# One 512-column matmul over the high and low half of the activations, and token sections of 256 and 264

## The chip, the cores and the metric

The kernel runs on one core of a Trainium2 chip. Its time is the device time of one execution in microseconds (us). The core has a matmul engine (PE, whose weight loads are shown apart as PEld), a vector engine (DVE), a scalar engine (ACT), a GpSimd engine (POOL) and a queue engine (SP) that starts the DMA transfers. All of them follow their own instruction lists and wait for each other by semaphores.

## The reference, cut to what matters

One layer of a hybrid decoder is run for a prompt of 512 tokens and for 8 sample tokens that share its weights. Everything is float32.

```
h = RMSNorm(x);  z = h @ w_in           # 2048 -> 7168 columns, split among branches
pool branch:   windowed means of u, a 128x128 map per group, gated by silu
dil branch:    3 groups x 4 heads of dilated window attention, QK-norm, merged by denominators
mem branch:    4-head cross-attention into 256 memory tokens (mem @ w_mem_kv, QK-norm)
x = x + concat(branches) @ w_out        # 1536 -> 2048 columns
```

The caches of the sample tokens are copied to the outputs, shifted by one position (most of the DMA traffic).

## The kernel before

The tokens lie along the free axis: 512 prompt and 8 sample tokens are NT = 520 columns, and 128 channels fill the partitions. A *job* computes 128 output channels for all 520 tokens: 56 jobs for w_in (16 blocks of 128 input channels each, "k-steps"), 8 jobs for the memory's keys and values (16 k-steps, 256 columns), and 16 jobs for w_out (12 k-steps).

Float32 precision comes from a split. A weight block `w` and an activation block `x` are each written as a high part, rounded to the matmul engine's reduced float32 (`F32R`), and a low part, the rest. A k-step adds up three products: high weight by high activation, high weight by low activation, low weight by high activation. The tokens are cut into two sections of HT = 260 columns (`SEC`), each with its own PSUM bank, so a k-step has six matmuls of 260 columns, each with its own weight load. The reduced-float32 matmuls have the tile names `whi` and `wlo` in their rows; the attention's own matmuls are in full float32 and run as two passes each.

The weights come as raw tiles (`wraw`) by DMA. `emit_split` cuts them a quarter of a job at a time (4 k-steps): ACT writes `whi`, DVE writes `wlo` from the raw tile and `whi`, both 128x512. Four such pairs are kept, so a quarter is split about three quarters of a job before PE needs it. The activation halves are the tiles `xh0..15` and `xl0..15`; the output projection writes its split activations into the same tiles (`split_y`). The memory's split activations use tiles that are free at that time (`y0..y11`, `S`, `kp`).

When a job's sums are done they are read out of PSUM one k-step into the next job (`flush_pend`, `evac`): per section one DVE instruction, sum times `rs_x` (the RMS factor) for w_in, or sum plus the residual for w_out (`o_evac`, `run_last`), times `rs_m` for the memory. Two PSUM tiles of two banks each (`psum_m`) take turns, so a readout has a whole job of time. The tile framework makes waits by whole tiles: in `run_last`, whose two sections run one after the other in one PSUM tile, the second section's first matmul waits for the readout of the first.

The order of everything is written by the kernel's own planner when it is built. A model of the engines' clocks (`Clock`) is advanced by every instruction; after each k-step `tick` gives the attention, normalization and sample tasks their next pieces as long as the modelled DVE and ACT backlog is under 2.5 us. So the DVE list mixes the weight splits, the readouts and the attention's arithmetic, in one fixed order, and an instruction that waits holds up all that stand behind it. POOL does the sums over partitions (`partition_all_reduce`).

The whole program: load and scale x while jobs 0 and 1 run; four jobs of memory queries and two more; the memory stage (8 jobs, some 45 to 55 us, up to about 155 us); 50 more w_in jobs with the attention of the four heads beside them; 16 output jobs.

Of the kernel before, what the change touches and what calls it, by code (L numbers as in the profile page):

```python
# [10 lines left out]
F32 = mybir.dt.float32  # L11
# [7 lines left out]
P = 128  # L19
# [4 lines left out]
NT = SEQ + NS  # L24
HT = NT // 2
ML = 256
# [88 lines left out]
def trunk(ctx, tc, nc, I, O):  # L115
# [88 lines left out]
    def mm(out, lhsT, rhs, start, stop):  # L204
        nc.tensor.matmul(out, lhsT=lhsT, rhs=rhs, start=start, stop=stop)  # L205
        n = nfree(rhs)
        d = 2 * max(0.107, n / 1200.0) if lhsT.dtype == F32 else max(0.107, (n + 6) / 2400.0)
        ck.use("pe", d, [lhsT, rhs], [out])

    def tr(out, in_):  # L210
# [97 lines left out]
    ysm = st([P, NH, NS], "ysm")  # L308
    xh = [st([P, NT], f"xh{k}", dt=F32R) for k in range(KB)]
    xl = [st([P, NT], f"xl{k}", dt=F32R) for k in range(KB)]  # L310
    Y = {}
# [95 lines left out]
    def run_jobs(group, each=None, before=None):  # L407
        accs = {}
        for j in group:
            _, _, _, sections, _, wide = jobs[j]  # L410
            if wide:
                t = psum_m()
                accs[j] = [t[:, s, 0:c1 - c0] for s, (c0, c1) in enumerate(sections)]
            else:
                need("psb", len(sections))
                accs[j] = [psum_b()[:, 0:c1 - c0] for c0, c1 in sections]
                if len(sections) == 2:
                    accs[j].append(None)
        nkb = jobs[group[0]][1]
        cur = {}  # L420
        for k in range(nkb):
            if before:
                before(k)
            for j in group:
                _, _, lhs, sections, _, _ = jobs[j]
                if k % 4 == 0:
                    cur[j] = split_t.pop((j, k))
                whi, wlo = cur[j]
                mh, ml = lhs(k)
                for a, b, w, m in ((0, 0, whi, mh), (0, 1, whi, ml), (1, 0, wlo, mh)):  # L430
                    for s, (c0, c1) in enumerate(sections):
                        mm(accs[j][s], w[:, k % 4, :], m[:, c0:c1],
                           start=(k == 0 and a == 0 and b == 0), stop=(k == nkb - 1 and a == 1))
            if each:
# [8 lines left out]
        for j in group:  # L443
            pend.append((len(jobs[j][3]) == 2, lambda j=j: jobs[j][4](accs[j])))

    def run_last(j):

# [3 lines left out]
        for s, (c0, c1) in enumerate(SEC):  # L451
            acc = t[:, s, 0:c1 - c0]
            for k in range(KO):
                whi, wlo = split_t[j, k - k % 4]
                mh, ml = xs(k)
                for n, (w, m) in enumerate(((whi, mh), (whi, ml), (wlo, mh))):
                    mm(acc, w[:, k % 4, :], m[:, c0:c1], k == 0 and n == 0, k == KO - 1 and n == 2)
                if k == 0:
                    flush_pend()
            d_tt(o[:, c0:c1], acc, xr[:, c0:c1], ALU.add)  # L460
            store(O["o_y"][j - first_o][:, c0:c1], o[:, c0:c1])
# [33 lines left out]
    def mem_evac(i):  # L495
        h = i % NH

        def key(acc):
            z = kmem[h]
            d_tt(z, acc[0], rs_m, ALU.mult)  # L500
            give("psb")
# [6 lines left out]
        def value(acc):  # L508
            need("vt")
            z = row("vt", 2)[:, 0:ML]  # L510
            d_tt(z, acc[0], rs_m, ALU.mult)
            give("psb")
# [17 lines left out]

    SEC = ((0, HT), (HT, NT))

    def evac(z, acc):
        for s, (c0, c1) in enumerate(SEC):
            d_tt(z[:, c0:c1], acc[s], rs_x[:, c0:c1], ALU.mult)
        if len(acc) > 2:
# [334 lines left out]
    def pool_task(c, u):  # L871
# [25 lines left out]
        for s, (c0, c1) in enumerate(SEC):  # L897
            mm(a[s][:, 0:HT], poolw[c], nt_[:, c0:c1], True, True)
        give("vt", 2)
# [4 lines left out]
        for s, (c0, c1) in enumerate(SEC):  # L904
            yv = Y[c][:, c0:c1]
            d_stt(yv, a[s][:, 0:HT], gains[:, GC_PS + c:GC_PS + c + 1], yv, ALU.mult, ALU.mult)
        give("psb", 2)
# [26 lines left out]
    def o_evac(m):  # L934
        def f(acc):
            xr = xres.pop(m)
            o = row("tmp", 3)
            for s, (c0, c1) in enumerate(SEC):
                d_tt(o[:, c0:c1], acc[s], xr[:, c0:c1], ALU.add)
            store(O["o_y"][m], o)  # L940
# [5 lines left out]

    xs = lambda k: (xh[k], xl[k])

# [13 lines left out]
    for i in range(NM):  # L962
        job(I["w_mem"][i], KB, lambda k: (memt[k // 2][0][:, k % 2, :], memt[k // 2][1][:, k % 2, :]),
            ((0, ML),), mem_evac(i), False)
# [32 lines left out]
    with tc.manual_schedule():  # L997
# [62 lines left out]
        def mem_prep():  # L1060
# [10 lines left out]
            for i in range(8):  # L1071
                r = raw.pop(i)
                mh = st([P, 2, ML], f"y{i}", 1, F32R)
                if i < 4:
                    ml = st([P, 2, ML], f"y{8 + i}", 1, F32R)
                elif i < 7:
                    if i == 4:
                        mls = st([P, 3, 2, ML], "S", 1, F32R)
                    ml = mls[:, i - 4]
                else:  # L1080
                    ml = st([P, 2, ML], "kp", 1, F32R)
                for s in range(2):
                    k = 2 * i + s
                    g = gains[:, GC_M + k:GC_M + k + 1]
                    act(mh[:, s, :], r[:, s, :], AF.Copy, scale=g)
                    d_stt(ml[:, s, :], r[:, s, :], g, mh[:, s, :].bitcast(F32), ALU.mult, ALU.subtract)
                if i == 0:
                    act(acc_m, r, AF.Square)
                else:
# [4 lines left out]
                    give("tmp")  # L1094
                memt[i] = (mh, ml)
                fetch(i + 4)
# [167 lines left out]
```

## Time and profile before

| what | value |
|---|---|
| median of 3 runs | 928.36 us (927.41 to 928.66) |
| the profiled execution's own time | 927.97 us |
| its span, first to last instruction | 925.7 us |
| PE busy / DVE busy / ACT busy / POOL busy | 893.5 / 666.8 / 393.2 / 311.3 us |
| matmuls recorded | 7208 |
| mean granted TensorE clock | 0.992 of full speed |

"Busy" counts the time in which an engine has at least one instruction in work. Matmuls overlap one another, so a busy PE says only that it has work; how fast it goes is read from how far apart the matmuls start. The columns of the stretch table are the busy times of the engines in one stretch, each with its count of instructions, then the granted clock (1.00 is 2.4 GHz, 0.50 is 1.2 GHz), the busy share of the DMA engines and GB/s.

### The profile page before, as it was taken

To read this page: it belongs to the slowest core of one execution; us is meant where nothing else is said; L and a number is where in the kernel's file an instruction comes from. 1 tells how busy PE (TensorE), PEld (TensorE's weight loads), DVE (VectorE), ACT (ScalarE), POOL (GpSimd) and SP (SyncE) were. 2 spreads that over 40 slices of the span, in tenths; PEclk is the share of its full clock that TensorE was granted. 3 is DMA by queue.
4 is the path that set the end of the run, shared out by engine and by line. 5 is a ranking of instruction groups with operands and counts; after the bars stand their busy time and mean duration, and the time that the engine had idled before them with its cause. 6 is when DMAs were issued, how large, how long until landed. Compare 5 with 4: busy or idle time off the path is not lost.

```text
span 925.7 us, 18086 instructions
## 1 busy us (share of the span) xinstructions
PE 893.5 (97%) x7208; PEld 878.0 (95%) x7208; DVE 666.8 (72%) x1218; ACT 393.2 (42%) x785; POOL 311.3 (34%) x109
## 2 busy tenths in 40 slices
PE   5789998999999999999999999999999999999998
PEld 5689888999999999999999999999999999999998
DVE  7947898846776886798857996798766999533331
ACT  6336565443453453443434454245542535222220
POOL 4612525515333742372422743355323520000000
PEclk9889999999999999999999999999999999999999
DMA  7553356897777686659987689676986757699631
GB/s 241 172 180 130 114 190 193 269 355 236 239 243 249 215 283 198 219 185 309 334 263 257 225 289 337 220 252 214 337 301 210 268 169 252 227 391 320 234 117 47
DMA packets 64643, 219.52 MB, mean 237 GB/s; under 512 B 8488, under 2 KB 22696, under 8 KB 62376
## 3 DMA queue, kind: packets, MB, share of 16 engines
q1 hardware_dynamic: 64560, 218.39, 70.0%
q8 instruction: 56, 0.92, 0.4%
q14 instruction: 27, 0.22, 0.1%
HBM read 200.32 MB, written 106.25 MB: 331 GB/s over the span
## 4 chain that ended last, share of the span: by engine, by line
PE 75%; DVE 6%; ACT 1%; issue 1%; ACTq 0%
PE psm L205 70%; PE psb L205 4%; DVE wlo L164 2%; DVE sv L187 1%; DVE mx L164 1%; PE psb L211 1%; ACT sk L154 0%; DVE sz L164 0%; ACT whi L154 0%; DVE sy L164 0%; DVE qk L164 0%; DVE smx L183 0%; DVE vt L164 0%; DVE smx L168 0%; ACT ss L154 0%
## 5 line engine op out<-in xcount | busy, mean ns | idle before, releaser
L205 PE MATMUL psm<-xh,whi 128*128 128x260 f32 x2120 | 439.6, 288 | 10.2 <-ACT whi L154 7.1
L205 PE MATMUL psm<-xl,whi 128*128 128x260 f32 x2120 | 431.7, 284 | 9.2 <-DVE xl L168 8.7
L205 PE MATMUL psm<-xh,wlo 128*128 128x260 f32 x2120 | 431.6, 284 | 2.3 <-DVE wlo L164 2.3
L164 DVE TENSOR_TENSOR wlo<-wraw,whi 128x512 fp32r<-128x512 f32 x304 | 257.5, 857 | 219.6 <-ACT whi L154 212.8
L154 ACT ACTIVATE whi<-wraw 128x512 fp32r<-128x512 f32 x304 | 188.8, 628 | 403.6 <-PE psm L205 347.7
L205 PEld LDWEIGHTS psm<-xh,whi 128*128 128x128 f32 x2120 | 330.9, 190 | 16.7 <-ACT whi L154 7.1
L205 PEld LDWEIGHTS psm<-xl,whi 128*128 128x128 f32 x2120 | 329.3, 190 | 10.7 <-DVE xl L168 9.8
L205 PEld LDWEIGHTS psm<-xh,wlo 128*128 128x128 f32 x2120 | 330.2, 190 | 2.8 <-DVE wlo L164 2.7
L197 POOL PARTITION_ALL_REDUCE sk<-sk x32 | 132.6, 4145 | 145.0 <-DVE sk L164 105.6
L197 POOL PARTITION_ALL_REDUCE sq<-sq x32 | 104.6, 3276 | 137.8 <-ACT sq L154 137.8
L197 POOL PARTITION_ALL_REDUCE mx<-mx x17 | 44.3, 2605 | 84.8 <-DVE mx L164 82.8
L154 ACT ACTIVATE tmp<-tmp 128x520 f32<-128x520 f32 (+2 forms) x76 | 46.4, 610 | 16.6 <-DVE sq L168 14.4
L154 ACT ACTIVATE sk<-sk,smx 128x256 f32<-128x256 f32 (+1 forms) x64 | 35.2, 550 | 16.5 <-DVE smx L168 14.8
L205 PE MATMUL psb<-y,wlo 128*128 128x256 f32 x128 | 37.0, 289 | 5.2 <-DVE wlo L164 5.0
L205 PE MATMUL psb<-y,whi 128*128 128x256 f32 x192 | 41.1, 282 | 0.9 <-ACT whi L154 0.9
L168 DVE SCALAR_TENSOR_TENSOR qk<-qk,gains_r,sq 128x520 f32<-128x520 f32 x28 | 38.4, 1370 | 1.0
L205 PEld LDWEIGHTS psb<-y,whi 128*128 128x128 f32 x192 | 31.6, 188 | 1.1 <-ACT whi L154 1.1
L154 ACT ACTIVATE sq<-qk 128x520 f32<-128x520 f32 x28 | 17.5, 633 | 34.6 <-DVE qk L164 34.6
L205 PEld LDWEIGHTS psb<-y,wlo 128*128 128x128 f32 x128 | 24.0, 188 | 7.3 <-DVE wlo L164 7.3
L201 POOL TENSOR_TENSOR rsx<-rsx,y 128x520 f32<-128x520 f32 x15 | 24.5, 1633 | 12.4 <-DVE y L164 11.2
L187 DVE CUSTOM_DVE_ANT_1 sv<-sv,sk,sy 128x384 f32<-128x384 f32 x32 | 27.3, 892 | 0.6
L183 DVE TENSOR_REDUCE smx<-sk 128x2 f32<-128x512 f32 (+1 forms) x32 | 25.9, 810 | 0.0
(126 smaller groups left out, 701.5 us busy)
## 6 DMA issues: line engine op xcount, KB each, us to landing
o_cache<-cache SPq DMA_DIRECT2D x88, 712.0 KB, 7.3
wraw<-w_in SPq DMA_DIRECT2D x108, 512.0 KB, 5.3
o_cache<-cache SPq DMA_DIRECT2D x24, 584.0 KB, 6.5
vn<-xT SPq DMA_DIRECT2D x32, 260.0 KB, 4.6
wraw<-w_mem SPq DMA_DIRECT2D x16, 512.0 KB, 3.7
wraw<-w_out SPq DMA_DIRECT2D x14, 512.0 KB, 4.2
o_zero<-zero SPq DMA_DIRECT2D x6, 1024.0 KB, 7.4
sk<-dks SPq DMA_DIRECT2D x16, 384.0 KB, 4.9
```

Source lines behind the costliest of these rows:

```text
L154: nc.scalar.activation(out=out, in_=in_, func=func, scale=scale, bias=bias, **kw)
L164: nc.vector.tensor_tensor(out=out, in0=in0, in1=in1, op=op)
L168: nc.vector.scalar_tensor_tensor(out=out, in0=in0, scalar=scalar, in1=in1, op0=op0, op1=op1)
L183: nc.vector.tensor_reduce(out=out, in_=in_, op=op, axis=axis)
L187: nc.vector.tensor_tensor_reduce(out=out, in0=in0, in1=in1, scale=1.0, scalar=init, op0=op0, op1=op1, accum_out=accum)
L197: nc.gpsimd.partition_all_reduce(t, t, P, op)
L201: nc.gpsimd.tensor_tensor(out=out, in0=in0, in1=in1, op=op)
L205: nc.tensor.matmul(out, lhsT=lhsT, rhs=rhs, start=start, stop=stop)
L211: nc.tensor.transpose(out, in_, ident)
```

## The change

The two halves of an activation block lie in one tile, `xs2[k]` of shape [128, 2, 520], and the memory's in one tile per k-step, `memt[k]`. The sections are 256 and 264 columns. For a section of 256 columns a new helper `mm3` issues one matmul of the high weight over both halves at once: 2 x 256 moving columns, written to 512 columns of one PSUM bank. The low weight's product of 256 columns is added to the first 256 of them. The section of 264 has the three matmuls of before. A k-step has five matmuls (512, 256, 264, 264, 264) and the same 1560 columns. The memory's k-step has two (512 and 256) in place of three.

The two halves of such a sum are added when they are read (`read_acc`): with a residual by two DVE instructions; with a factor by an ACT copy of the second half out of PSUM, a DVE addition of the first half, and a DVE multiplication. The planner's price of a reduced-float32 matmul changes from max(0.107, (n+6)/2400) to (n+28)/2400 us.

```diff
-HT = NT // 2
+LO = 256
...
-        d = 2 * max(0.107, n / 1200.0) if lhsT.dtype == F32 else max(0.107, (n + 6) / 2400.0)
+        d = 2 * max(0.107, n / 1200.0) if lhsT.dtype == F32 else (n + 28) / 2400.0
         ck.use("pe", d, [lhsT, rhs], [out])
+
+    def mm3(accs, whi, wlo, m2, sections, first, last):
+
+
+        for acc, (c0, c1) in zip(accs, sections):
+            n = c1 - c0
+            if n == LO:
+                mm(acc, whi, m2[:, :, c0:c1], first, False)
+                mm(acc[:, 0:n], wlo, m2[:, 0, c0:c1], False, last)
+            else:
+                mm(acc[:, 0:n], whi, m2[:, 0, c0:c1], first, False)
+                mm(acc[:, 0:n], whi, m2[:, 1, c0:c1], False, False)
+                mm(acc[:, 0:n], wlo, m2[:, 0, c0:c1], False, last)
 
     def tr(out, in_):
         nc.tensor.transpose(out, in_, ident)
...
     ysm = st([P, NH, NS], "ysm")
-    xh = [st([P, NT], f"xh{k}", dt=F32R) for k in range(KB)]
-    xl = [st([P, NT], f"xl{k}", dt=F32R) for k in range(KB)]
+    xs2 = [st([P, 2, NT], f"x{k}", dt=F32R) for k in range(KB)]
+    xh = [t[:, 0, :] for t in xs2]
+    xl = [t[:, 1, :] for t in xs2]
     Y = {}
     QKB = 8
     VNB = 6
...
                 t = psum_m()
-                accs[j] = [t[:, s, 0:c1 - c0] for s, (c0, c1) in enumerate(sections)]
+                accs[j] = [t[:, s, :] for s in range(len(sections))]
             else:
                 need("psb", len(sections))
-                accs[j] = [psum_b()[:, 0:c1 - c0] for c0, c1 in sections]
+                accs[j] = [psum_b() for _ in sections]
                 if len(sections) == 2:
                     accs[j].append(None)
         nkb = jobs[group[0]][1]
...
-                mh, ml = lhs(k)
-                for a, b, w, m in ((0, 0, whi, mh), (0, 1, whi, ml), (1, 0, wlo, mh)):
-                    for s, (c0, c1) in enumerate(sections):
-                        mm(accs[j][s], w[:, k % 4, :], m[:, c0:c1],
-                           start=(k == 0 and a == 0 and b == 0), stop=(k == nkb - 1 and a == 1))
+                mm3(accs[j], whi[:, k % 4, :], wlo[:, k % 4, :], lhs(k), sections, k == 0, k == nkb - 1)
             if each:
                 each(k)
             if k % 4 == 3:
...
 
+    def read_acc(out, acc, other, op):
+
+        n = out.shape[-1]
+        if n != LO:
+            d_tt(out, acc[:, 0:n], other, op)
+        elif op == ALU.add:
+            d_tt(out, acc[:, 0:n], other, op)
+            d_tt(out, out, acc[:, n:2 * n], op)
+        else:
+            act(out, acc[:, n:2 * n], AF.Copy)
+            d_tt(out, out, acc[:, 0:n], ALU.add)
+            d_tt(out, out, other, op)
+
...
     def run_last(j):
 
         t = psum_m()
         xr = xres.pop(j - first_o)
         o = row("tmp", 3)
         for s, (c0, c1) in enumerate(SEC):
-            acc = t[:, s, 0:c1 - c0]
+            acc = t[:, s, :]
             for k in range(KO):
                 whi, wlo = split_t[j, k - k % 4]
-                mh, ml = xs(k)
-                for n, (w, m) in enumerate(((whi, mh), (whi, ml), (wlo, mh))):
-                    mm(acc, w[:, k % 4, :], m[:, c0:c1], k == 0 and n == 0, k == KO - 1 and n == 2)
+                mm3([acc], whi[:, k % 4, :], wlo[:, k % 4, :], xs(k), ((c0, c1),), k == 0, k == KO - 1)
                 if k == 0:
                     flush_pend()
-            d_tt(o[:, c0:c1], acc, xr[:, c0:c1], ALU.add)
+            read_acc(o[:, c0:c1], acc, xr[:, c0:c1], ALU.add)
             store(O["o_y"][j - first_o][:, c0:c1], o[:, c0:c1])
 
 
...
             z = kmem[h]
-            d_tt(z, acc[0], rs_m, ALU.mult)
+            read_acc(z, acc[0], rs_m, ALU.mult)
             give("psb")
 
             def after():
...
 
 
-    SEC = ((0, HT), (HT, NT))
+    SEC = ((0, LO), (LO, NT))
 
     def evac(z, acc):
         for s, (c0, c1) in enumerate(SEC):
-            d_tt(z[:, c0:c1], acc[s], rs_x[:, c0:c1], ALU.mult)
+            read_acc(z[:, c0:c1], acc[s], rs_x[:, c0:c1], ALU.mult)
         if len(acc) > 2:
             give("psb", 2)
 
...
             for s, (c0, c1) in enumerate(SEC):
-                d_tt(o[:, c0:c1], acc[s], xr[:, c0:c1], ALU.add)
+                read_acc(o[:, c0:c1], acc[s], xr[:, c0:c1], ALU.add)
             store(O["o_y"][m], o)
             if len(acc) > 2:
                 give("psb", 2)
...
 
-    xs = lambda k: (xh[k], xl[k])
+    xs = lambda k: xs2[k]
 
     def zjob(cb, done, wide=True):
         job(I["w_in"][cb], KB, xs, SEC, done, wide)
...
-        job(I["w_mem"][i], KB, lambda k: (memt[k // 2][0][:, k % 2, :], memt[k // 2][1][:, k % 2, :]),
+        job(I["w_mem"][i], KB, lambda k: memt[k],
             ((0, ML),), mem_evac(i), False)
     first_q = len(jobs)
     for h in range(NH):
...
                 r = raw.pop(i)
-                mh = st([P, 2, ML], f"y{i}", 1, F32R)
-                if i < 4:
-                    ml = st([P, 2, ML], f"y{8 + i}", 1, F32R)
-                elif i < 7:
-                    if i == 4:
-                        mls = st([P, 3, 2, ML], "S", 1, F32R)
-                    ml = mls[:, i - 4]
-                else:
-                    ml = st([P, 2, ML], "kp", 1, F32R)
                 for s in range(2):
                     k = 2 * i + s
+                    if k < 12:
+                        m2 = st([P, 2, ML], f"y{k}", 1, F32R)
+                    elif k < 15:
+                        if k == 12:
+                            mls = st([P, 3, 2, ML], "S", 1, F32R)
+                        m2 = mls[:, k - 12]
+                    else:
+                        m2 = st([P, 2, ML], "kp", 1, F32R)
                     g = gains[:, GC_M + k:GC_M + k + 1]
-                    act(mh[:, s, :], r[:, s, :], AF.Copy, scale=g)
-                    d_stt(ml[:, s, :], r[:, s, :], g, mh[:, s, :].bitcast(F32), ALU.mult, ALU.subtract)
+                    act(m2[:, 0, :], r[:, s, :], AF.Copy, scale=g)
+                    d_stt(m2[:, 1, :], r[:, s, :], g, m2[:, 0, :].bitcast(F32), ALU.mult, ALU.subtract)
+                    memt[k] = m2
                 if i == 0:
                     act(acc_m, r, AF.Square)
                 else:
...
                     give("tmp")
-                memt[i] = (mh, ml)
                 fetch(i + 4)
                 ck.last = max(ck.pe, ck.written[raw[i + 1].tensor.name]) if i < 7 else ck.last
                 yield
```

In `run_last` each section's loop now calls `mm3` with that one section.

The matmul engine's list, in an ordinary w_in job; the rows of one k-step and the start of the next, before and after (`x2` joins equal rows; psm is the PSUM tile, xh, xl and x the activations):

```order
L205 MATMUL psm_7694<-xh_23_86,whi_7576 128x260 x2
L205 MATMUL psm_7694<-xl_39_102,whi_7576 128x260 x2
L205 MATMUL psm_7694<-xh_23_86,wlo_7577 128x260 x2
L205 MATMUL psm_7694<-xh_24_87,whi_7576 128x260 x2
L205 MATMUL psm_7694<-xl_40_103,whi_7576 128x260 x2
```

```order
L205 MATMUL psm_6792<-x_32_95,whi_6728 128x512
L205 MATMUL psm_6792<-x_32_95,wlo_6729 128x256
L205 MATMUL psm_6792<-x_32_95,whi_6728 128x264 x2
L205 MATMUL psm_6792<-x_32_95,wlo_6729 128x264
L205 MATMUL psm_6792<-x_33_96,whi_6728 128x512
```

Six matmuls have become five, and the low weight is wanted after one matmul instead of four.

DVE's list around the readout of the same w_in job (a q or k of the second head's attention), before and after (qk is the readout's target, psm the sums, rsx the RMS factor; mx, S, sk, smx belong to the attention and the sample tokens):

```order
L164 TENSOR_TENSOR wlo_4695<-wraw_4322,whi_4694 128x512
L164 TENSOR_TENSOR wlo_4724<-wraw_4322,whi_4723 128x512
L164 TENSOR_TENSOR qk_4747<-psm_4579,rsx_71 128x260 x2
L164 TENSOR_TENSOR sk_4597<-sk_4597,qs_81 128x768
L164 TENSOR_TENSOR mx_4751<-S_4348 128x512
```

```order
L164 TENSOR_TENSOR mx_4221<-S_3891 128x512
L164 TENSOR_TENSOR mx_4221<-mx_4221,S_3891 128x4x64 x3
L164 TENSOR_TENSOR mx_4221<-mx_4221,S_3891 128x4x32
L183 TENSOR_REDUCE smx_4241<-sk_3413 128x2
L168 SCALAR_TENSOR_TENSOR smx_4241<-smx_4241,nself_3884 128x2
L164 TENSOR_TENSOR wlo_4265<-wraw_3872,whi_4264 128x512
L164 TENSOR_TENSOR qk_4282<-qk_4282,psm_4120 128x256
L164 TENSOR_TENSOR qk_4282<-qk_4282,rsx_71 128x256
L164 TENSOR_TENSOR qk_4282<-psm_4120,rsx_71 128x264
L164 TENSOR_TENSOR sk_4163<-sk_4163,qs_81 128x768
```

The readout has three DVE rows instead of two (its ACT copy stands in ACT's list), and the attention's `mx` rows have moved ahead of it. DVE has 80 instructions more in all (56 + 8 + 16), ACT 64 more (56 + 8).

The end of DVE's list, the readouts of the last two jobs, before and after (tmp is the result tile, vn the residual):

```order
L164 TENSOR_TENSOR tmp_10902<-psm_10804,vn_10722 128x260 x2
L164 TENSOR_TENSOR wlo_10927<-wraw_10681,whi_10926 128x512
L164 TENSOR_TENSOR wlo_10955<-wraw_10746,whi_10954 128x512
L164 TENSOR_TENSOR tmp_10987<-psm_10895,vn_10815 128x260 x2
L164 TENSOR_TENSOR tmp_10983<-psm_10982,vn_10906 128x260 x2
```

```order
L164 TENSOR_TENSOR tmp_9908<-psm_9828,vn_9759 128x256
L164 TENSOR_TENSOR tmp_9908<-tmp_9908,psm_9828 128x256
L164 TENSOR_TENSOR tmp_9908<-psm_9828,vn_9759 128x264
L164 TENSOR_TENSOR tmp_9905<-psm_9904,vn_9839 128x256
L164 TENSOR_TENSOR tmp_9905<-tmp_9905,psm_9904 128x256
L164 TENSOR_TENSOR tmp_9905<-psm_9904,vn_9839 128x264
```

The first section of the last job is read by two instructions, and the second section's matmuls stand behind both.

## Rows read from the trace of the kernel before

**Rows 1.** The page, part 1: busy time of each engine, share, instructions.

```profile
PE 893.5 (97%) x7208; PEld 878.0 (95%) x7208; DVE 666.8 (72%) x1218; ACT 393.2 (42%) x785; POOL 311.3 (34%) x109
```

**Rows 2.** Chain that ended last: start us, length us, engine, tile, instructions.

```profile
156.06 48.29 PE psm L205 x402
...
805.99 111.35 PE psm L205 x929
...
917.36 0.44 DVE tmp L164
...
917.84 4.58 PE psm L205 x36
...
922.45 0.43 DVE tmp L164
```

**Rows 3.** Timeline of PE, memory stage: start us, us, instruction, count.

```profile
121.47 0.28 PE L205 MATMUL psb<-y,wlo 128*128 128x256 f32 x1
...
122.89 0.28 PE L205 MATMUL psb<-y,wlo 128*128 128x256 f32 x1
```

**Rows 4.** Timeline of PE, at half clock.

```profile
34.67 0.64 PE L205 MATMUL psm<-xh,wlo 128*128 128x260 f32 x2
...
37.27 0.42 PE L205 MATMUL psm<-xh,wlo 128*128 128x260 f32 x1
```

**Rows 5.** Stretches: us, PE, PEld, DVE, ACT, POOL busy (count), clock, DMA, GB/s.

```profile
34.30:37.40 3.10, 3.10 (x15) 3.10 (x16) 3.10 (x4) 2.95 (x5) 2.52 (x2) 0.50 0.76 272
...
100.00:160.00 60.00, 52.77 (x420) 50.10 (x420) 55.28 (x91) 34.31 (x68) 29.46 (x9) 1.00 0.54 176
394.00:450.00 56.00, 55.22 (x456) 54.86 (x455) 49.63 (x85) 26.39 (x58) 27.32 (x8) 1.00 0.77 261
520.00:560.00 40.00, 40.00 (x335) 40.00 (x334) 38.36 (x67) 21.49 (x46) 17.51 (x6) 1.00 0.87 296
604.00:660.00 56.00, 54.53 (x451) 54.17 (x450) 49.12 (x95) 26.92 (x60) 26.99 (x7) 1.00 0.72 252
740.00:790.00 50.00, 50.00 (x412) 49.76 (x411) 45.96 (x114) 21.44 (x45) 4.75 (x1) 1.00 0.64 214
800.00:900.00 100.00, 100.00 (x838) 100.00 (x836) 33.53 (x62) 22.73 (x36) 0.00 (x0) 1.00 0.75 265
```

**Rows 6.** Chain, 203 to 208 us: a full-float32 matmul of 512 columns.

```profile
204.35 0.86 PE psb L205 x2
```

**Rows 7.** Waits of PE: who for whom, us in total, times, longest.

```profile
PE psm L205 <- DVE xl L168: 8.7, 5, 2.4
...
PE psb L205 <- DVE wlo L164: 5.0, 8, 1.4
PE psm L205 <- DVE wlo L164: 2.3, 2, 1.5
...
PE psm L205 <- DVE tmp L164: 0.5, 1, 0.5
```

**Rows 8.** Groups by form: shapes, count, busy us, mean ns, idle before.

```profile
L164 DVE TENSOR_TENSOR wlo<-wraw,whi 128x512 fp32r<-128x512 f32 x304 | 257.5, 857 | 219.6 <-ACT whi L154 212.8 <-PE psb L205 2.8 <-DMA wraw<-w_out 2.2
...
L164 DVE TENSOR_TENSOR qk<-psm,rsx 128x260 f32<-128x260 f32 x62 | 23.3, 419 | 0.0
...
L154 ACT ACTIVATE y<-vn,gains 128x256 fp32r<-128x256 f32 x16 | 7.2, 494 | 0.0
...
L164 DVE TENSOR_TENSOR S<-S,mx 128x256 f32<-128x256 f32 x12 | 4.3, 415 | 0.0
```

**Rows 9.** Tile wlo on DVE: ns min/median/max.

```profile
L164 DVE TENSOR_TENSOR wlo<-wraw,whi x304: 674/691/3732, 7.0 to 910.6; 128x512 fp32r<-128x512 f32 x152
```

**Rows 10.** Chain, 630 to 660 us.

```profile
637.01 2.80 DVE wlo L164
...
644.44 0.69 DVE wlo L164
...
645.18 14.92 PE psm L205 x122
```

**Rows 11.** Groups by form, DVE, 800 to 926 us.

```profile
L164 DVE TENSOR_TENSOR wlo<-wraw,whi 128x512 fp32r<-128x512 f32 x40 | 27.5, 692 | 67.3 <-ACT whi L154 63.8 <-DMA wraw<-w_out 2.2 <-PE psb L205 1.3
```

More of the change, by code (lines that the diff above doesn't have):

```diff
@@ L510, in value @@
             z = row("vt", 2)[:, 0:ML]
-            d_tt(z, acc[0], rs_m, ALU.mult)
+            read_acc(z, acc[0], rs_m, ALU.mult)
             give("psb")
@@ L897, in pool_task @@
         for s, (c0, c1) in enumerate(SEC):
-            mm(a[s][:, 0:HT], poolw[c], nt_[:, c0:c1], True, True)
+            mm(a[s][:, 0:c1 - c0], poolw[c], nt_[:, c0:c1], True, True)
         give("vt", 2)
@@ L905, in pool_task @@
             yv = Y[c][:, c0:c1]
-            d_stt(yv, a[s][:, 0:HT], gains[:, GC_PS + c:GC_PS + c + 1], yv, ALU.mult, ALU.mult)
+            d_stt(yv, a[s][:, 0:c1 - c0], gains[:, GC_PS + c:GC_PS + c + 1], yv, ALU.mult, ALU.mult)
         give("psb", 2)
```

## The prediction

> **What bounds the kernel now.** I read the page's busy times first, then the chain of waits, then the stretches, then who waits for whom. PE is busy 893.5 of 925.7 us, the next engine, DVE, 666.8 [rows 1]. The chain shows why that is no idle figure: from 156 us on it is matmuls end to end, 402 in 48.29 us, and near the end 929 in 111.35 us [rows 2]. That is 120.1 and 119.9 ns from one 260-column matmul to the next. At the full clock of 2.4 GHz the 260 columns alone are 108.3 ns, so each matmul has 11.5 ns on top. A step of six takes 6 x 119.9 = 719 ns.
>
> Three places are not paced by PE. At the start it waits for x (8.7 us in five waits for `xl`) [rows 7]. In the memory stage DVE is busy 55.28 of 60 us and PE waits eight times, 5.0 us, for `wlo` [rows 5, 7]. And in four stretches of the attention (394 to 450, 520 to 560, 604 to 660, 740 to 790 us) DVE is busy 88 to 96% of the time [rows 5]: there a weight split comes late, as at 644.44, right after which PE goes on at 645.18 [rows 10]. Over 800 to 900 us DVE has only 33.53 us of work [rows 5].
>
> **The change, part by part.** I start from the profiled execution, 927.97 us; the median is 0.4 above it.
>
> *PE after the memory stage.* Columns per k-step stay at 6 x 260 = 512 + 256 + 3 x 264 = 1560. Matmuls go from six to five. What this saves depends on what the 11.5 ns belong to, and no row before shows a 512-column matmul of this kind.
> - If they belong to the matmul, whatever its length, a step saves 11.5 ns. The 256-column matmuls speak for it: 12 of them in 122.89 - 121.47 = 1.42 us, 118.3 ns each, or 106.7 + 11.6 [rows 3].
> - If they belong to the column, PE streams 260/119.9 = 2.17 columns per ns, and the step saves nothing. 256/118.3 = 2.16 fits this as well; four columns are too few to tell the two apart.
> - If a longer stream hides them, 512 columns cost little over 213.3 ns. The nearest row is the full-float32 matmul, whose two passes of 512 columns at half that column rate take 0.86 us, 430 ns each against 426.7, so 3.3 ns on top [rows 6]. At half clock, too, the 260 columns take 12 in 2.60 us, 216.7 ns, with nothing on top [rows 4, 5]. The step would save 11.5 + 8.2 = 19.7 ns.
>
> I take the first, the middle one: it is what both lengths at this clock and in this number format give with one constant. After the memory stage come 50 jobs of 16 steps and 16 of 12, 992 steps: **-11.4 us** (bounds 0 and -19.5). Of the 96 steps before it I count half, since PE waits for x in the first two jobs: -0.5. The first matmul of a step now needs `xl` too; while x arrives that is worth up to 1 us and I put it at nothing, since the next `xh` is what PE would wait for.
>
> *The memory stage.* Its 128 steps lose one matmul of three, 1.5 us of PE, but DVE paces it. DVE gets one more addition or multiplication per readout, at 0.42 us [rows 8], eight times 3.4 us; between all of it on the path and a gain of 1.5 us I take **+1.5**.
>
> *The readouts of the w_in jobs.* DVE has three instructions for two. The nearest rows are 419 ns for one that reads PSUM and 415 ns for a 256-column one inside SBUF [rows 8], so 56 x 0.42 = 23 us more of DVE. ACT gets 56 copies of at most 494 ns each [rows 8]; ACT is busy 393 of 926 us, and the copy stands behind a `whi` split that DVE's list must wait for anyway. Outside the four stretches the cover is the split's lead of three quarters of a job (8.6 us), and 23 us do not reach the end. Inside them DVE has no room: a stretch of 40 to 56 us is some four jobs, so DVE needs 4 x 0.42 = 1.7 us longer while PE wants to be 4 x 0.18 = 0.7 us earlier, 2.4 us of lateness each, 9.6 in four. In two of them a split already comes too late (2.3 us of PE waits [rows 7]), so there it counts in full; in the others part of the lead is still there. I take **+5** (0 to 10). Standing behind a late instruction on DVE is always the next `wlo`, and behind that PE.
>
> *The planner.* Its price for a 260-column matmul rises by 8%, and the attention's pieces move against the matmuls, as the `mx` rows before the readout show. The same work stands in the same jobs to within one; I add nothing and allow 3 us either way.
>
> *The output jobs and the end.* 16 more additions, 6.7 us, lie in DVE's idle time from 800 us on. One is on the path: in the last job the second section waits for the readout of the first, 0.44 us and then PE [rows 2], and this is now two instructions: **+0.4**. The last readout stays one.
>
> Sum: 927.97 - 11.4 - 0.5 + 1.5 + 5 + 0.4 = 923.0. On the level of the median that is 923.4; I say 923.
>
> One rule of the Trainium skill speaks against the readout's form. `wlo`, which reads two operands from SBUF, takes 691 ns in the median but up to 3732, 857 in the mean over the kernel and 692 where POOL does nothing [rows 8, 9, 11]. "SBUF — State Buffer", section "Who interferes with whom", says that a DVE instruction with two SBUF inputs and a GpSimd instruction that reads SBUF exclude each other for their whole length. These rows agree. By the rule the added multiplication can be held up so; the addition from PSUM cannot.
>
> **The rivals.**
> - *The longer stream hides the cost of a start.* For: the full-float32 passes and the half-clock rows. Against: the short matmul has its weights loaded beside it as well. 927.97 - 19.5 - 0.9 + 1.5 + 7 + 0.4 = 916.5, say 917 (the lateness in the stretches grows with a faster PE). A rule comes out close to it: "TensorE: Matmul & The Clock Gate", section "Back-to-back issue gap", gives N/2.4 + 2.5 ns, so 215.8 for 512 columns. But it gives 110.8 for 260, where the trace has 119.9, so the rule does not hold for this format as it stands.
> - *The cost is by the column.* PE gains nothing, and what DVE was given remains: 927.97 + 1.5 + 4 + 0.4 = 933.9, say 934, slower than before. For: both lengths fit 2.17 columns per ns. Against: at half clock the columns run at exactly 1.2 per ns, so the array as such has no such loss; what feeds it would have to be short.
> - *The added multiplication runs into POOL.* In the four attention stretches, POOL is busy up to half of the time, and one split there took 2.80 us in place of 0.69 [rows 5, 10]. If one readout per job is held up by 2.1 us, 16 jobs get 34 us of DVE, of which half on the path is 17 instead of 5: 935. It eats the whole gain from 10 us of lateness on (11.4 + 0.5 - 1.5 - 0.4). Against: the readouts' multiplications would all have to meet an all-reduce.
>
> **How the numbers follow.** The forecast (one start saved, the stretches take back part) has 0.58, the hidden start 0.14, the cost by the column 0.20, the collision with POOL 0.08. What can be told from no change is 0.2%, so faster is below 926.5 and slower above 930.2. The forecast's own range is 917 to 929, from lateness and planner; of it 0.43 is faster, 0.11 the same, 0.04 slower. The hidden start gives 0.13 and 0.01; the cost by column 0.03 same and 0.17 slower; POOL 0.03 and 0.05. Together 0.56, 0.18, 0.26. The range 913 to 935 leaves out one end of the hidden start and the worst of the stretches.
>
> **What would show it.** In the profile after: the start-to-start of a step in the output jobs (707.5 ns by the forecast, 699 if hidden, 719 by the column), and of the 512-column matmul alone (225, 217 or 236 ns). PE's waits for `wlo`: some 6.5 us more than the 7.3 of now in all. The added multiplication: 0.42 us, or over 0.6 in the mean if POOL holds it up. The forecast is wrong if the 512-column matmul is not near 225 ns, or if the waits for `wlo` do not grow.

## The result, and the profile after

The changed kernel takes 934.81 us (933.98 to 936.58, 4 runs) against 928.51 us (927.41 to 929.76, 4 runs): ratio 1.0066, 95% interval 1.0054 to 1.0078. It is 0.7% slower where I forecast 0.5% faster. The profiled execution has 934.42 us and a span of 932.5 us, 6.8 us more than before.

The page's busy times of the kernel after, in the columns of [rows 1]:

```profile
PE 894.7 (96%) x5992; PEld 820.2 (88%) x5992; DVE 694.8 (75%) x1298; ACT 408.7 (44%) x849; POOL 310.9 (33%) x109
```

1216 matmuls have gone and PE's busy time has not fallen; DVE has 28 us more, ACT 15.5. The rate of PE is read from starts. First rows of two output jobs, eight jobs apart, in PE's timeline (start us, us, instruction, count), of the kernel after and then of the kernel before:

```profile
841.74 0.40 PE L205 MATMUL psm<-x,whi 128*128 128x512 f32 x1
...
910.62 0.40 PE L205 MATMUL psm<-x,whi 128*128 128x512 f32 x1
```

```profile
835.20 0.40 PE L205 MATMUL psm<-xh,whi 128*128 128x260 f32 x2
...
904.22 0.40 PE L205 MATMUL psm<-xh,whi 128*128 128x260 f32 x2
```

68.88 us after and 69.02 before for 8 x 12 steps: 717.5 ns a step against 719.0. One matmul less saves 1.5 ns, not 11.5.

What PE waits for, after (us in total, times, longest), beside [rows 7]:

```profile
PE psb L205 <- DVE wlo L164: 7.6, 8, 2.2
...
PE psm L205 <- DVE x L164: 4.9, 3, 2.0
...
PE psm L205 <- DVE wlo L164: 2.2, 7, 0.5
PE psm L205 <- DVE tmp L164: 1.2, 2, 1.0
```

The waits for `wlo` are 9.8 us instead of 7.3. The row `x L164` is new in this size, 4.9 us in three waits: these are the splits of the last attention results, between w_in and w_out (called the passage below). The prediction has the need of both halves at the start alone, where x arrives, and puts it at nothing.

The stretches after, in the columns of [rows 5]:

```profile
100.00:160.00 60.00, 52.04 (x294) 43.56 (x293) 57.38 (x102) 39.24 (x82) 25.30 (x10) 1.00 0.49 167
394.00:450.00 56.00, 55.41 (x379) 51.18 (x379) 43.13 (x84) 28.06 (x65) 25.97 (x7) 1.00 0.75 268
...
604.00:660.00 56.00, 55.38 (x384) 51.29 (x383) 45.17 (x87) 27.64 (x68) 28.34 (x8) 1.00 0.69 245
```

In the memory stage DVE has 57.4 of 60 us. In the two attention stretches it is less busy than before, though it was given work: the planner's order is another one, and the fixed windows hold other pieces of the attention. So before and after can't be compared stretch by stretch, and the experiments below separate the order from the operations.

DVE and ACT by form, after (shapes, count, busy us, mean ns, idle before):

```profile
L164 DVE TENSOR_TENSOR qk<-qk,rsx 128x256 f32<-128x256 f32 x32 | 15.5, 485 | 1.1
...
L164 DVE TENSOR_TENSOR qk<-qk,psm 128x256 f32<-128x256 f32 x31 | 12.8, 412 | 0.0
...
L154 ACT ACTIVATE qk<-psm 128x256 f32<-128x256 f32 x31 | 11.2, 365 | 0.0
```

The prices of the single instructions were right: 0.41 us for the addition, 0.49 for the multiplication, 0.37 for the copy.

The end of the chain, after:

```profile
923.64 0.43 DVE tmp L164
...
924.09 0.43 DVE tmp L164
...
924.57 4.69 PE psm L205 x36
...
929.28 0.43 DVE tmp L164
```

Between the two sections of the last job 0.93 us pass, 0.48 in [rows 2]: the +0.4 of the forecast.

### The profile page after: what moved, and what is told of

Its sections match the earlier page's. It is cut to its first block, busy times and chain, and to the rows that moved or that the text cites. A ratio compares the mean times of both kernels' runs of the same rounds, so it can differ in the third digit from the quotient of the medians.

```text
span 932.5 us, 15796 instructions
## 1 busy us (share of the span) xinstructions
PE 894.7 (96%) x5992; PEld 820.2 (88%) x5992; DVE 694.8 (75%) x1298; ACT 408.7 (44%) x849; POOL 310.9 (33%) x109
## 4 chain that ended last, share of the span: by engine, by line
PE 68%; DVE 18%; ACT 5%; issue 3%; DMA 1%; SPq 0%; DVEq 0%; ACTq 0%
PE psm L205 61%; PE psb L205 7%; DVE wlo L164 6%; DVE sv L187 2%; DVE mx L164 2%; ACT whi L154 1%; ACT tmp L154 1%; DVE vt L164 1%; ACT sk L154 1%; DVE tmp L168 1%; DVE smx L183 1%; DVE sq L168 1%; DVE qk L164 1%; DVE y L168 1%; DMA vn<-xT 1%
## 5 line engine op out<-in xcount | busy, mean ns | idle before, releaser
L205 PE MATMUL psm<-x,whi 128*128 128x264 f32 (+1 forms) x3180 | 782.5, 327 | 24.3 <-DVE x L168 8.4
L205 PE MATMUL psm<-x,wlo 128*128 128x256 f32 (+1 forms) x2120 | 603.6, 285 | 2.3 <-DVE wlo L164 2.2
L205 PEld LDWEIGHTS psm<-x,whi 128*128 128x128 f32 x3180 | 530.6, 190 | 78.7 <-DVE x L168 9.5
L205 PEld LDWEIGHTS psm<-x,wlo 128*128 128x128 f32 x2120 | 403.6, 190 | 8.6 <-DVE wlo L164 5.8
L164 DVE TENSOR_TENSOR wlo<-wraw,whi 128x512 fp32r<-128x512 f32 x304 | 256.2, 853 | 193.5 <-ACT whi L154 188.0
L205 PE MATMUL psb<-y,whi 128*128 128x512 f32 x96 | 34.4, 396 | 0.2 <-ACT whi L154 0.2
L205 PE MATMUL psb<-y,wlo 128*128 128x256 f32 x96 | 27.6, 288 | 6.4 <-DVE wlo L164 6.2
L168 DVE SCALAR_TENSOR_TENSOR qk<-qk,gains_r,sq 128x520 f32<-128x520 f32 x28 | 30.8, 1099 | 1.0
L154 ACT ACTIVATE tmp<-sq,eps 128x520 f32<-128x520 f32 (+1 forms) x32 | 22.2, 693 | 10.4 <-POOL sq L197 10.3
L164 DVE TENSOR_TENSOR tmp<-psm,vn 128x256 f32<-128x256 f32 (+1 forms) x30 | 12.7, 422 | 17.0 <-PE psm L205 9.4
L168 DVE SCALAR_TENSOR_TENSOR sq<-tmp,tmp 128x520 f32<-128x520 f32 (+1 forms) x32 | 24.0, 749 | 1.1
```

Of the source, the lines that this page charges most:

```text
L154: nc.scalar.activation(out=out, in_=in_, func=func, scale=scale, bias=bias, **kw)
L164: nc.vector.tensor_tensor(out=out, in0=in0, in1=in1, op=op)
L168: nc.vector.scalar_tensor_tensor(out=out, in0=in0, scalar=scalar, in1=in1, op0=op0, op1=op1)
```

## The experiments

Ratios are to the kernel before, timed beside the run on the same chip (928.5 to 929.3 us).

**What a matmul costs.** Behind the last output job, the changed kernel issues ten series of 36 matmuls that nothing reads but a copy: reduced float32 of several widths, the strided 2 x 256 form, and bf16.

```diff
+        for i, (nm, n) in enumerate(forms):
+            for r in range(36):
+                k = r % KO
+                w = split_t[last, k - k % 4][0][:, k % 4, :]
+                m = flat[k][:, 0:n] if n else xs2[k][:, :, 0:256]
+                mm(o, w, m, r == 0, r == 35)
+        for i, n in enumerate((260, 512)):
+            for r in range(36):
+                mm(o, xb[r % 2][:, 512:640], xb[(r + 1) % 2][:, 0:n], r == 0, r == 35)
```

> The changed kernel with ten series of 36 matmuls behind its last job, nothing else changed: reduced float32 with 260, 256, 264, 384, 512 contiguous, 2 x 256 strided, 128 and again 512 columns, then bfloat16 with 260 and 512. Cost by the column (theory 1): start to start follows N/2.2 plus 2 to 3 ns, so 120, 118.5, 122, 177, 234, 234 and, for 512, no more than 2 ns between contiguous and strided. One start cost per matmul (the forecast's step): 171.5 ns at 384 and 225 at 512. A strided read that costs extra (theory 2): 512 contiguous at 225, 2 x 256 at 234. If the four bytes per column are what slows the stream, bfloat16 runs at 111 and 216 ns; if not, at 120 and 234.

PE's timeline of that run, one row from inside each series: 260, 256, strided 512, contiguous 512, and bf16 260 and 512:

```profile
929.82 3.40 PE L205 MATMUL psm<-x,whi 128*128 128x260 f32 x27
934.25 3.45 PE L205 MATMUL psm<-x,whi 128*128 128x256 f32 x28
958.30 6.90 PE L205 MATMUL psm<-x,whi 128*128 128x512 f32 x29
970.45 6.89 PE L205 MATMUL psm<-x,whi 128*128 128x512 f32 x29
978.11 3.61 PE L205 MATMUL psm<-vn,vn 128*128 128x260 bf16 x31
982.32 6.85 PE L205 MATMUL psm<-vn,vn 128*128 128x512 bf16 x31
```

A row runs from the first start to the last end, and one matmul alone reads 0.28 us (256 or 260 columns) or 0.40 (512). From start to start: (3.40 - 0.28) / 26 = 120.0 ns for 260 columns, 117.4 for 256, 232.1 for the strided 512 and 231.8 for the contiguous. From 256 to 512 that is 0.447 ns per column and 3.0 ns on top, and the series of 264 and 384 columns, 120.9 and 175.0 ns, lie on the same line (128 columns don't, at 111.6). The cost goes by the column, at 2.24 columns per ns; of the 11.5 ns that I gave to the start, three belong to it. A bf16 matmul alone reads 0.27 and 0.38 us, so bf16 takes 111.3 and 215.7 ns. The Trainium skill, "TensorE: Matmul & The Clock Gate", section "Back-to-back issue gap", gives N/2.4 + 2.5 as the gap of an isolated matmul at the full clock, which is 110.8 and 215.8: the bf16 rows, 36 in a row, agree all the same, the reduced float32 rows don't.

**The planner's price alone.** Two kernels: before with the new price of a matmul, after with the old one.

```diff
-        d = 2 * max(0.107, n / 1200.0) if lhsT.dtype == F32 else max(0.107, (n + 6) / 2400.0)
+        d = 2 * max(0.107, n / 1200.0) if lhsT.dtype == F32 else (n + 28) / 2400.0
```

> The kernel before, with the changed kernel's price for a reduced-float32 matmul in the planner and nothing else. Theory A, the loss of 5 to 6 us at the passage to the output jobs comes from the order that the new price gives: 933 to 935 us, with the two jobs at the passage taking some 25 us in place of 21.6. Theory B, it comes from the longer readouts: 928 us as before, 21.6 us there.

> The changed kernel with the old price. Theory A: the two jobs at the passage fall back to some 21.6 us and the whole to about 928. Theory B: it stays at 934 to 935, 25 us there.

936.91 us, 1.0088 (1.0073 to 1.0103), and 944.39 us, 1.0166 (1.0151 to 1.0182). Both lie above what either theory gave. With the other price either kernel gets a worse order. A number that no engine sees moves the time by 8 to 10 us, through what the planner makes of it.

**One half read, order left free.** After, every 256-column sum read by one instruction.

```diff
-        if n != LO:
+        if True:
             d_tt(out, acc[:, 0:n], other, op)
```

> The changed kernel without the second half's addition: each sum is read by one DVE instruction per section, so the product of high weight and low activation is left out for the first 256 columns. It lacks the 80 DVE and 64 ACT instructions of the change. Theory A: still 932 to 935, the loss at the passage stays. Theory B: 927 to 929, the loss is gone. A third theory, that the readouts cost lateness all along the attention (the forecast's +5): a gain of 4 to 5 us spread over 390 to 790 us, where the trace of the changed kernel shows none.

939.79 us, 1.0121 (1.0104 to 1.0138): slower with less work, and outside all three theories. The planner sees fewer instructions and makes a third order, so this run tells nothing of the readouts.

**Operations and order apart.** From here the order is written out: a table says after which k-step which task gets its next piece, taken once from the kernel before and once from the kernel after.

```diff
-        budget = ck.pe + 1.2
-        for task in list(tasks):
-            if task[0] > ck.pe:
-                continue
-            if ck.pe > budget or busy():
-                break
+        snap = list(tasks)
+        for c in next(plan):
+            task = snap[int(c, 36)]
             if not advance(task):
                 tasks.remove(task)
```

Three runs: the new operations in the old order, the old operations in the new order, and the first of them with one half read.

> The changed kernel, with the points at which the planner advanced the tasks written out from the kernel before: every engine's list stands in the order of before, with the new matmuls and the longer readouts in their places. Theory order (the new matmuls and readouts are about even, and the loss is the new order of the tasks): 926 to 930 us, the two jobs at the passage to the output jobs take some 21.6 us. Theory operations (the readouts cost it, wherever they stand): 933 to 936.

> The kernel before, with the tasks advanced at the points of the changed kernel: its old matmuls and readouts in the new order. Theory order: 934 to 937 us, some 25 us for the two jobs at the passage. Theory operations: 927 to 930.

> As the changed kernel in the old order, without the second half's addition in the readouts (the product of high weight and low activation is left out for the first 256 columns): 80 DVE and 64 ACT instructions less. Theory order: within 1.5 us of the run with them, since DVE's additions lie beside matmuls. Theory operations: 4 to 6 us below it. The forecast's term (+5 in the attention stretches, +1.5 in the memory stage): 6 below it, spread over 100 to 160 and 390 to 790 us.

| | old order | new order |
|---|---|---|
| old operations | 928.7 (before) | 925.21, 0.9959 (0.9946 to 0.9971) |
| new operations, one half read | 929.24, 1.0004 (0.9995 to 1.0013) | 924.68, 0.9957 (0.9945 to 0.9968) (next) |
| new operations | 948.46, 1.0204 (1.0177 to 1.0231) | 934.81, 1.0066 (1.0054 to 1.0078) (after) |

The theory that the order had cost the time fell: the new order is worth 3.5 us, and the old operations in it beat both kernels. The operations cost 20 us in the old order and 10 in the new; 20 is more than any of the theories gave. PE's waits of the new operations in the old order:

```profile
PE psm L233 <- DVE wlo L192: 9.2, 8, 2.6
...
PE psb L233 <- DVE wlo L192: 7.7, 10, 1.9
```

16.9 us for `wlo` against 7.3 [rows 7]. That order was made for a DVE with less to do. In the profiled run PE also stood at half clock three times, some 10 us in all, at 142, 162 and 432 us, which by half of it is an estimated 5 of the 20 us; the kernel before has no low clock between 100 and 925 us.

**Which readout, and which part of it.** In the new order: no second half read at all; the second half left out of the 56 w_in readouts only; and the same with ACT's copy kept and the multiplication still waiting for it, so that only DVE's addition is gone.

```diff
             read_acc(z[:, c0:c1], acc[s], rs_x[:, c0:c1], ALU.mult)
...
+            if c1 - c0 == LO:
+                act(z[:, c0:c1], acc[s][:, LO:2 * LO], AF.Copy)
+            d_tt(z[:, c0:c1], acc[s][:, 0:c1 - c0], rs_x[:, c0:c1], ALU.mult)
```

> The changed kernel's matmuls in the changed kernel's own order of tasks, written out, but every readout of a 256-column section is one instruction as before (left out: the second half, the product of the high weight with the low activation for those columns). If the readouts cost what the changed kernel lost and the matmul's saving is the 1.4 ns per step seen in the output jobs, this comes out 1 us below the old operations in this order: about 924 us (0.995 of before). If instead the merged matmul itself, or the first matmul's earlier need of the low half, costs time in this order, it lands at 928 or above.

> The changed kernel in its own order; only the 56 w_in readouts leave the second half out (so the high weight times low activation of those columns), the memory's 8 and the output's 16 still read both halves. Theory w_in: the attention's and the passage's lateness comes from these 56, and 6 to 7 of the 9.6 us go, so about 928 us. Rival, the memory stage and the output jobs carry it: it stays within 2 us of the changed kernel, 933 to 935 us.

> As the run before it, but the scalar engine's copy of the second half stays in the w_in readouts and the multiplication behind it waits for the copy; only the vector engine's addition is gone (its sum is left out). Theory vector engine: the added 0.42 us on the full vector engine is the price, so this is within 1 us of the run without the copy. Rival, the wait for the scalar engine: the vector engine stands behind a copy that stands in the scalar engine's list, and this run stays 3 us or more above the run without the copy, near the changed kernel.

924.68 us, 0.9957 (0.9945 to 0.9968); 928.35 us, 0.9990 (0.9981 to 1.0000); 927.28 us, 0.9990 (0.9981 to 0.9998). The copy and the wait for ACT cost nothing that the intervals show. The 56 additions on DVE, 0.41 us each or 23 us, cost 7 (1.0066 - 0.9990 of 928.5). Without the addition the multiplication also reads PSUM in place of a second SBUF operand, so these runs alone can't tell the addition from a multiplication held up beside POOL. The trace of the changed kernel can: two of its 56 multiplications were held, 1.9 us at 333 us and 1.6 us at 267 us, between jobs 16 and 34, where the table below shows no step. The readouts of the memory and the output jobs cost the other 3 (0.9990 - 0.9957).

Who waited for the tile `wlo` (us, times), in the kernel after and then in the run without the addition:

```profile
  PEld psm L205: 5.8, 10
  PE psm L205: 2.2, 7
```

```profile
  PEld psm L232: 1.6, 3
  PE psm L232: 0.5, 1
```

Without the addition the weight loads of the w_in jobs wait three times instead of ten. The starts of jobs in the profiled runs (us, the first matmul of each job, read from the timeline) show where:

| start of job | 6 | 16 | 34 | 38 | 44 | 46 | 52 | 56 | 64 | 67 | end |
|---|---|---|---|---|---|---|---|---|---|---|---|
| after | 98.6 | 177.8 | 407.5 | 454.8 | 531.5 | 556.0 | 632.8 | 680.1 | 780.7 | 815.8 | 932.5 |
| without the addition, less after | -2.5 | -3.5 | -3.7 | -5.1 | -5.1 | -6.5 | -6.5 | -7.9 | -8.3 | -7.4 | -7.5 |
| one half read, less after | -1.8 | -4.4 | -4.5 | -5.9 | -5.9 | -7.4 | -7.4 | -8.8 | -9.1 | -7.6 | -8.2 |
| old operations, less after | -1.4 | -3.8 | -3.1 | -4.3 | -3.9 | -5.3 | -5.1 | -6.3 | -6.3 | -9.3 | -9.5 |

The addition's lateness comes in steps of 1.3 to 1.5 us at jobs 34 to 38, 44 to 46 and 52 to 56, and 3.5 us before job 16. Three of the four stretches of [rows 5] are there; in the fourth it is 0.3. The steps are firm: the run with the ten series, which is the changed kernel up to its end, keeps its distance to it within 0.1 us from job 16 to job 64. The 3.5 us are less so: that run is 0.5 us earlier at job 16 and 1.7 at job 2, and two runs of the old operations in the new order (the second is below) differ by 1.8 us at job 16. One of these steps, in the chain of the kernel after:

```profile
426.92 0.34 DVE qk L164
...
427.62 0.44 DVE qk L164
...
428.08 0.64 ACT sq L154
428.72 0.63 ACT tmp L154
...
430.59 0.62 ACT whi L154
...
431.24 0.70 DVE wlo L164
...
431.99 28.25 PE psm L205 x195
```

The longer readout of `qk` on DVE holds ACT's `sq`, ACT's list brings the `whi` split late, `wlo` follows it, and PE goes on when it is there.

**The passage.** The last column but one has something else: from job 64 to job 67 the old operations take 32.1 us, the new ones 35.2, with one half read 36.7. So it isn't the readouts. PE's timeline there, after, with the idle time in brackets:

```profile
791.81 0.50 PE L205 MATMUL psm<-x,whi 128*128 128x512 f32 x1 [0.92 <-DVE x L164]
...
799.20 0.50 PE L205 MATMUL psm<-x,whi 128*128 128x512 f32 x1 [1.96 <-DVE x L164]
...
803.77 0.50 PE L205 MATMUL psm<-x,whi 128*128 128x512 f32 x1 [1.99 <-DVE x L164]
```

and with the old operations in the same order:

```profile
785.11 0.51 PE L232 MATMUL psm<-xl,whi 128*128 128x260 f32 x2 [0.23 <-DVE xl L191]
...
791.41 0.51 PE L232 MATMUL psm<-xh,whi 128*128 128x260 f32 x2 [1.09 <-ACT xh L181]
792.14 0.51 PE L232 MATMUL psm<-xl,whi 128*128 128x260 f32 x2 [0.23 <-DVE xl L191]
...
795.74 0.51 PE L232 MATMUL psm<-xh,whi 128*128 128x260 f32 x2 [1.25 <-ACT xh L181]
796.47 0.51 PE L232 MATMUL psm<-xl,whi 128*128 128x260 f32 x2 [0.23 <-DVE xl L191]
```

The old k-step starts with the high half, which ACT has written some 0.7 us before DVE's low half, and has two matmuls' work (0.5 us in the rows) before it needs the other. The merged matmul comes first and needs both. Waits of 3.0 us have become 4.9. After them the clock fell (stretches, columns of [rows 5]; after, then the old operations):

```profile
800.00:804.60 4.60, 2.61 (x16) 2.06 (x15) 1.64 (x3) 0.64 (x1) 0.00 (x0) 1.00 0.00 0
804.60:807.80 3.20, 3.20 (x14) 2.91 (x13) 1.38 (x2) 1.26 (x2) 0.00 (x0) 0.50 0.15 49
```

```profile
785.00:796.40 11.40, 8.57 (x56) 7.36 (x56) 7.93 (x22) 2.91 (x5) 0.00 (x0) 1.00 0.54 197
796.40:800.00 3.60, 3.53 (x29) 3.53 (x30) 1.40 (x3) 1.27 (x2) 0.00 (x0) 1.00 0.20 34
```

3.2 us at 1.2 GHz, after a stretch in which PE was busy 2.61 of 4.60 us, cost half of that, 1.6. With the shorter waits it stayed at 2.4. In the run with one half read, whose passage is the longest, the low clock begins earlier and lasts some 10 us:

```profile
784.00:796.00 12.00, 8.08 (x41) 6.45 (x41) 6.72 (x19) 1.90 (x3) 0.00 (x0) 0.80 0.37 137
796.00:800.00 4.00, 4.00 (x17) 3.71 (x16) 1.38 (x2) 1.26 (x2) 0.00 (x0) 0.50 0.19 24
```

All five profiled runs with the merged matmul in this order have a low clock here, for 3 to 10 us, and neither of the two with the old operations has one. In the run with the ten series, the same program as the changed kernel up to its end, it lasts longer and the passage takes 36.4 us. In the old order, where the waits are 1.1 us with the merged matmul and 0.5 before, the clock stays up and the passage is 1.4 to 1.8 us longer (31.68 and 32.09 us against 30.25).

Whether the wait comes from the merged matmul, or from the two halves lying in one tile, two runs tell: the old operations with that edit alone, in either order.

```diff
-    xh = [st([P, NT], f"xh{k}", dt=F32R) for k in range(KB)]
-    xl = [st([P, NT], f"xl{k}", dt=F32R) for k in range(KB)]
+    xs2 = [st([P, 2, NT], f"x{k}", dt=F32R) for k in range(KB)]
+    xh = [t[:, 0, :] for t in xs2]
+    xl = [t[:, 1, :] for t in xs2]
```

> The old operations in the changed kernel's order (925.2 us in an earlier run), with one edit: the high and low half of an activation block lie in one tile, the matmuls and readouts stay as they were. Theory one tile: a matmul that reads the high half now waits for the write of the low half too, which is 0.7 us later at each of the three late splits of the passage to the output jobs; so PE's waits there go from 3.0 us in all to about 4.9, and the kernel becomes 1.5 to 3 us slower, 927 to 928 us. Rival, the wait comes only with the merged matmul, which needs both halves: no change, 925 us.

> The kernel before with the one edit of one tile for both halves, in the old order written out. Theory one tile: the changed operations lengthened the passage (output job pair's start to the next job's) by 1.8 us in this order, 30.2 to 32.1; if the tile does it, this is 1 to 3 us slower than before, 930 to 932 us. Rival, the merged matmul: no change from before, 928.9 us.

925.39 us, 0.9965 (0.9952 to 0.9977), and 928.24 us, 0.9995 (0.9985 to 1.0005): no change in either. PE's waits at the passage, in the new order:

```profile
PE psm L232 <- ACT x L181: 2.3, 2, 1.2
PE psm L232 <- DVE x L191: 0.7, 3, 0.2
```

They still part into the high half's and the low half's: within one SBUF tile the framework waits for the region that is read, not for the whole tile. What I said ahead of the prediction of waits by whole tiles is shown here for the PSUM tile of `run_last` alone. My theory of one tile fell; what is left is the merged matmul, which reads both halves. A k-step that puts the high half's other matmuls ahead of it was not tried.

## Why the prediction was wrong

In the same order and in the profiled runs, the new operations cost 932.54 - 923.02 = 9.52 us, and the order gave 2.69. The parts, from differences of the profiled runs above:

| part | forecast | measured | from |
|---|---|---|---|
| PE rate, up to job 64 and in the output jobs | -11.9 | -3.2 | one half read, less old operations |
| readouts, memory and output jobs (with the one at the end) | +1.9 | +1.3 (timed: 3) | w_in left out, less one half read |
| readouts, w_in: addition | +5 | +7.5 | after, less copy only |
| readouts, w_in: ACT's copy | 0 | -0.6 | copy only, less w_in left out |
| passage: merged matmul needs both halves | 0 | +4.5 (in the changed kernel +3.0 and +4.3) | one half read, less old operations |
| planner's order | 0 ± 3 | -2.7 | old operations in the new order, less before |
| sum | -5.0 | +6.8 | |

Two cautions. The profiled execution with one half read was the slowest of its five, 1.6 us above their median (926.25 against 924.68). By the medians that run is even with the old operations (0.9957 and 0.9959), which puts the passage nearer 3 us and the readouts of the memory and the output jobs nearer 3 as well. And the sum takes the order first, with the old operations; with the new ones the order is worth some 13 us (1.0204 - 1.0066).

*PE after the memory stage* is the step that failed: of the 11.4 us that it was to save, the runs show some 3. I said that the 11.5 ns belong to the matmul; by the series 8.5 of them go with the columns, and the 512-column matmul takes 232 ns, not 225. Columns at 2.24 per ns fit both lengths that I had, within about a nanosecond, and I took the other reading because at half clock the columns ran at exactly 1.2 per ns. That row was no argument: it shows a rate that holds at half clock, and what paces the columns at full clock no run here tells. By the series a step would still save 7.5 ns (720.0 to 712.5, the 264-column matmul put at 0.447 x 264 + 3.0 = 121.0). The kernel shows 1.5 in the output jobs, and in the w_in jobs 2.9 (the difference of the last two rows of the table of starts grows from 0.55 to 1.39 us over 18 jobs of 16 steps, unrounded). In the step of the output jobs the starts lie 233.9 ns apart for the 512 columns, 118.0 for the 256 and 122.5, 122.1 and 121.0 for the three of 264: nearly each takes a little more than in its series, 5 ns in all. Why a step of mixed widths gives back most of the saving is open.

*The w_in readouts* went as written in the attention, in place and mechanism: hidden outside the stretches, late in three of the four, and 4.7 us from job 16 to job 64 against 5. Two things were not in it: up to 3.5 us before the attention, less firm as said above, and that the cost depends on the order: all readouts together cost 19 us in the old one (1.0204 - 1.0004) and 10 in the new (1.0066 - 0.9957).

*The first matmul of a step now needs xl too*, I wrote, and put it at nothing, with the start of the kernel in view. The passage, where y arrives late as x does at the start, I did not look at; it cost 3.0 to 4.5 us, in waits and at half clock.

*The planner's order*: ±3 was a guess. The old operations took 925.2 to 936.9 us in three orders, the new ones 934.8 to 948.5 in three; that the order now made was a good one could not be read from the trace before.

*The collision with POOL* was small: 3.5 us of DVE in two places, as said above. DVE's rows of the tiles `qk` and `vt` (ns min/median/max), after:

```profile
L164 DVE TENSOR_TENSOR qk<-qk,rsx x32: 424/425/2324, 60.6 to 785.5; 128x256 f32<-128x256 f32 x32
L164 DVE TENSOR_TENSOR qk<-qk,psm x31: 406/412/417, 60.1 to 785.0; 128x256 f32<-128x256 f32 x31
...
L164 DVE TENSOR_TENSOR vt<-vt,rsx x12: 424/425/2016, 267.4 to 611.7; 128x256 f32<-128x256 f32 x12
```

Of these multiplications of two SBUF operands one is held in either tile, to 2.3 and 2.0 us, while POOL works on an all-reduce of `mx` (the second, too); the mean in `qk` is 485 ns, not over 600. The addition from PSUM is never held. The Trainium skill, "SBUF — State Buffer", section "Who interferes with whom", says that a DVE instruction with two SBUF inputs contends with a GpSimd instruction that reads SBUF, and that one with at most one, outside the two-port modes, does not contend; these rows agree.

Of the rivals, the cost by the column came out in its premise, and in size (934) by luck. Its working had 5.9 us for all readouts where 8.2 were measured, and nothing for the rate, the passage and the order, which happen to add up to no more than -1.4 us.

## What to carry to other kernels

Two lengths 4 columns apart can't tell a cost per instruction from a cost per column: measure the long form before building on it, and of the readings take the one that needs no constant. On a full engine an instruction costs its own time where the consumer waits, whatever the mean over the kernel says, and a merged instruction waits for the latest of what it merges, so look at every place where those operands arrive late. Where a planner writes the order, freeze the order first and then compare operations; else one measures the planner.

## What the hardware showed that I had not expected

- Reduced float32 streams 2.24 columns per ns at full clock, bf16 in the same run 2.4 (215.7 ns for 512 columns). A strided operand of 2 x 256 columns costs nothing over a contiguous one (232.1 and 231.8).
- Two waits of PE of 2.0 us were followed by 3.2 us at 1.2 GHz; with waits of 1.1 and 1.3 us at the same place the clock stayed at 2.4 GHz.
